# A hybrid attention step with split-precision projections: two projections at each side of the change of token groups made in pairs by halves of the contraction, and each weight load issued at its split

## The chip, the core and the metric

The program runs on one core of one Trainium2 chip, in one launch. The metric is the device time of one execution in microseconds (us). Three runs of the kernel before took 2360.5, 2361.33 and 2364.92 us; the median is 2361.33.

A core has five engines, each working through its own list of instructions in order: TensorE (PE in the profile, its weight loads PEld), VectorE (DVE), ScalarE (ACT), GpSimd (POOL) and SyncE (SP), which here only issues DMAs. An instruction that has to wait for a semaphore holds up all that stand behind it on the same engine.

## The reference

One layer over 1024 new prompt tokens and 128 sample tokens (8 streams of 16, each with 1024 cached keys and values), width 2048:

```python
h = rms_norm(x, norm_pre)
q_sb, k_sb, v_sb, gate_sb, q_r, k_r, v_r, gate_r = split(h @ w_in)   # 8 heads of 128 each
q_r, k_r = rope(q_r, pos), rope(k_r, pos) * HEAD_DIM ** -0.5
o_sb = stick_breaking(q_sb, k_sb, v_sb)      # strictly causal, over the cached keys too
o_r, state = retention(q_r, k_r, v_r, state) # chunks of 64, a decay of its own for each head
y_sb = head_rms_norm(o_sb) * silu(gate_sb)
y_r  = head_rms_norm(o_r) * silu(gate_r)
x = x + rms_norm(concat(y_sb, y_r) @ w_out, norm_post)
```

All is float32. Beside x, the new keys, values and retention states are returned.

## The kernel before, in words

**Split products.** TensorE multiplies float32 as three products of a faster format: each operand is cut in a high and a low part, and high x high, low x high and high x low are added up in the accumulator. ScalarE writes the high parts (`wh` of a weight, `mh` of the moving operand, line 138), VectorE the low parts (`wl`, `ml`, line 139). Before either can work, the raw block must have been loaded from memory: `wr` for a weight (four buffers), `mr` for an operand block (two buffers).

**Groups.** The 1152 tokens are taken in two groups. Group 0 is prompt tiles 0 to 3 and the sample tile: 640 columns, in pieces of 256 and 384. Group 1 is prompt tiles 4 to 7, 512 columns in one piece. All projections of group 0 for all eight heads come first, then all of group 1. A projection is named by what it makes and its head: q, k, v and sg (the gate) for stick-breaking, rq, rk, rv and rg for retention, so that sg7 is the last of group 0 and rq0, rk0, rv0 are the first three of group 1.

**One projection.** `project` (line 310) contracts 2048 rows in four quarters of four blocks of 128. For each quarter, called a piece here, one weight load of 256 KB is taken, split, and multiplied with that quarter of the operand: 12 products per piece and column range, 48 in all. rv and v have another form (`project_rows`: the tokens are the stationary side, the weight tiles are called `wrn`, `whn`, `wln` and the accumulators `accn`).

**The operand and its refill.** The operand of the running group stays on the chip in split form: four quarters, each with one buffer for its high and one for its low part. At the change of groups it is filled anew with group 1's normalised input, which lies in memory as `s_h`. `load_moving` (line 193) does that block by block: it issues the load of block k+1 on SP (line 199), then splits block k. A quarter can be overwritten only when the last product that reads its old content is done, and the next group's product on it waits until it is filled:

```python
            ahead = load(k + 1) if k + 1 < KT else None
            split(hi[q][:, j, at : at + n], lo[q][:, j, at : at + n], r)
```

Sixteen blocks are to be copied. sg7 takes four at its third and four at its fourth piece; rq0 takes four at its first and four at its second.

**What runs beside.** After each column of products `tick()` (line 170) lets one of the waiting jobs take a step: stick-breaking of the head before (scores `z`, `zc`, masks and scans), retention (`pa`, `pSs`), attention over the cache for the sample tokens, stores. A scheduler then settles the order of each engine's instructions, so that their place in the program is not the place in the code alone.

**Weights ahead.** `take_w` (line 278) hands out the next weight tile; it issues loads until three are in hand, the one handed out and two ahead (`W_AHEAD = 2`). The list `to_load` has them in the order of use.

**rope** (line 388) rotates rq and rk: ScalarE copies the two halves of the accumulator, swapped, into a tile `sw` (lines 392 and 393), which has one buffer, and VectorE does the arithmetic on it.

**Output.** After the heads, the output projection takes the tokens in three chunks of four panels each (`out_panel`, products in lines 1150 to 1152), with a weight load per block of 128 rows. In the third and fourth panels of a chunk the residual rows `xr` (1 MB a load, line 1197) are issued behind the newest weight load at every sixth block. The very last panel is 256 columns wide; the other 256 columns' weights have been kept on the chip before (`keep_last`, line 1176).

Of the kernel before, what the change touches and what calls it, by code (L numbers as in the profile page):

```python
# [10 lines left out]
F32R = mybir.dt.float32r  # L11
# [5 lines left out]
P = 128  # L17
# [35 lines left out]
W_AHEAD = 2  # L53
# [9 lines left out]
def tile_hybrid_step(  # L63
# [129 lines left out]
    def load_moving(mov, at, n, src):  # L193
# [10 lines left out]
        for k in range(KT):  # L204
# [14 lines left out]
            for s in (  # L219
# [5 lines left out]
    }  # L225

# [40 lines left out]
    loaded_w = []  # L267
    to_load = []
    for gi in range(2):
        for step, h in order[gi][1 - gi :]:  # L270
            if step != "ret":
                to_load += projection_loads(step, h)
# [10 lines left out]
    def load_w(first=None):  # L283
        for w in range(KT // WQ):
# [25 lines left out]
    def project(pieces, mov, loads=None, refill=()):  # L310
# [5 lines left out]
        return list(zip(acc, pieces))  # L316

# [51 lines left out]
    with ExitStack() as s1:  # L369
# [601 lines left out]
        class Head:  # L971
            def __init__(self, gi, h, last):
                self.gi, self.h, self.last = gi, h, last
                self.rest, self.ret = {}, {}
                self.sb_job = self.ret_job = None
# [13 lines left out]
            def do_rq(self):  # L989
                acc = project(self.g["pieces"], mov, run["loads"], (0, 1))  # L990
                run["loads"] = None
                if self.last:
                    drain(self.last.ret_job)
                self.ret["rq"] = rope(acc, "rq", *ropes)

            def do_rk(self):
                self.ret["rk"] = rope(project(self.g["pieces"], mov), "rk", *ropes)
# [15 lines left out]
            def do_q(self):  # L1013
# [11 lines left out]
                if self.sample:  # L1025
# [3 lines left out]
                    run["dec"] = Job(decode(self.h, qs, self.rest), D_DEC)  # L1029

            def do_k(self):
                acc = project(self.pieces, mov)
# [3 lines left out]
                ks = None  # L1036
# [4 lines left out]
                k2 = [kq.tile([P, NB_TOK], F32R, name=f"k{c}", tag=f"k{c}") for c in "hl"]  # L1041
                evac_split(acc, *k2)
                keys = [k2]
                if self.gi == 1:
# [4 lines left out]
                    keys = [old, k2]  # L1049
# [3 lines left out]
                    sb_branch(self.gi, self.tiles, self.h, self.q2, keys, kT, self.rest, ks), D_NAT[phase[0]]  # L1053
# [301 lines left out]
```

## Time and profile before

| | before |
|---|---|
| runs | 2360.5, 2361.33, 2364.92 us (median 2361.33) |
| the profiled execution: its time | 2362.25 us |
| its span, first to last instruction | 2359.5 us |
| mean granted TensorE clock | 0.997 |
| TensorE busy | 2316.6 us (98%) |
| VectorE, ScalarE, GpSimd busy | 1340.3, 895.2, 506.9 us |
| moved by DMA | 418.58 MB, mean 177 GB/s |

The views are of this one execution, and all their times count from the span's start. A row of a timeline gives start, length, engine, line, operation, out<-in, and in brackets the idle time of the engine just before with what ended it ("[3.08 <-ACT whn L138]": 3.08 us, ended by ScalarE's write of whn in line 138). A row of a windows table gives the stretch, its length and, for each engine, the busy time with its count, then the granted clock (1.00 is full), the share of the DMA engines that was busy, and GB/s. A row of groups gives busy time and the mean of one in ns.

### The profile page before, as it was taken

How to read it: one execution, taken by the hardware profiler on the slowest of the kernel's cores; microseconds unless marked ns; L12 is line 12 of the kernel's file. 1: busy time of each engine (PE TensorE's matmuls, PEld its weight loads, DVE VectorE, ACT ScalarE, POOL GpSimd, SP SyncE). 2: the span in 40 equal slices, each digit the busy share in tenths (PEclk: the TensorE clock that was granted, in tenths of full speed). 3: DMA queues.
4: the chain of work that ended last, by engine and by line, in shares of the span. 5: the costliest groups of instructions: out<-in, count | busy, mean ns of one | idle time of the engine just before them, and what ended most of it. 6: DMA issues, size and time to landing. Idle time of an engine off the chain costs nothing.

```text
span 2359.5 us, 39392 instructions
## 1 busy us (share of the span) xinstructions
PE 2316.6 (98%) x14256; PEld 2055.8 (87%) x14256; DVE 1340.3 (57%) x2689; ACT 895.2 (38%) x1926; POOL 506.9 (21%) x751
## 2 busy tenths in 40 slices
PE   7999999999999999999999999999999999999998
PEld 7999999999999999998788888888888877878887
DVE  7246564556556564557556656565665575564544
ACT  6323332333233332334343433434343444444342
POOL 3123241414223241414121211112122020010100
PEclk9999999999999999999999999999999999999999
DMA  7569686887969687797966555565565565765654
GB/s 248 151 151 232 161 187 168 190 193 174 203 147 219 170 185 178 181 209 186 231 171 151 149 159 152 140 152 156 147 160 148 146 173 187 232 213 185 202 176 132
DMA packets 697476, 418.58 MB, mean 177 GB/s; under 512 B 235072, under 2 KB 648256, under 8 KB 694848
## 3 DMA queue, kind: packets, MB, share of 16 engines
q1 hardware_dynamic: 635888, 321.12, 51.8%
q0 software_dynamic: 28304, 78.68, 13.5%
q10 hardware_dynamic: 33088, 16.26, 2.4%
q8 instruction: 111, 1.82, 0.3%
q14 instruction: 85, 0.70, 0.1%
HBM read 336.24 MB, written 79.69 MB: 176 GB/s over the span
## 4 chain that ended last, share of the span: by engine, by line
PE 84%; DMA 5%; DVE 4%; issue 4%; ACT 2%; POOL 1%; SPq 0%; ACTq 0%; DVEq 0%; POOLq 0%
PE acc L296 47%; PE accn L335 11%; PE accx L363 4%; PE a L1151 3%; PE a L1152 3%; PE a L1150 3%; PE pa L665 2%; PE z L632 2%; DMA mr<-s_y 2%; PE pd L801 1%; DMA mr<-s_ys 1%; PE zc L736 1%; DMA mr<-s_h 1%; DVE ml L139 1%; PE rs L823 1%
## 5 line engine op out<-in xcount | busy, mean ns | idle before, releaser
L139 DVE TENSOR_TENSOR wl<-wr,wh 128x512 fp32r<-128x512 f32 (+1 forms) x576 | 391.7, 683 | 514.9 <-ACT wh L138 499.9
L296 PE MATMUL acc<-mh,wl 128*128 128x256 f32 (+2 forms) x2304 | 662.9, 340 | 0.0
L296 PE MATMUL acc<-mh,wh 128*128 128x256 f32 (+2 forms) x2304 | 661.0, 339 | 0.7 <-ACT mh L138 0.7
L296 PE MATMUL acc<-ml,wh 128*128 128x256 f32 (+2 forms) x2304 | 660.4, 339 | 0.9 <-DVE ml L139 0.9
L138 ACT ACTIVATE wh<-wr 128x512 fp32r<-128x512 f32 (+1 forms) x576 | 358.8, 625 | 718.3 <-PE acc L296 397.9
L296 PEld LDWEIGHTS acc<-mh,wh 128*128 128x128 f32 x2304 | 421.4, 188 | 37.3 <-issue 6.6
L296 PEld LDWEIGHTS acc<-ml,wh 128*128 128x128 f32 x2304 | 421.3, 188 | 37.4 <-issue 6.2
L296 PEld LDWEIGHTS acc<-mh,wl 128*128 128x128 f32 x2304 | 421.1, 188 | 36.1 <-issue 7.8
L717 POOL DMA_DIRECT2D kc<-cache_sb_k x256 | 166.7, 655 | 284.4 <-DVE kcT L748 119.9
L335 PE MATMUL accn<-whn,mh 128*128 128x256 f32 x768 | 223.6, 292 | 3.1 <-ACT whn L138 3.1
L1151 PE MATMUL a<-wl,mh 128*128 128x512 f32 (+1 forms) x576 | 220.0, 382 | 2.7 <-DVE wl L139 2.5
L1150 PE MATMUL a<-wh,mh 128*128 128x512 f32 (+1 forms) x576 | 220.3, 383 | 1.8 <-ACT wh L138 1.7
L1152 PE MATMUL a<-wh,ml 128*128 128x512 f32 (+1 forms) x576 | 219.2, 381 | 0.0
L335 PE MATMUL accn<-wln,mh 128*128 128x256 f32 x768 | 217.7, 284 | 0.8 <-DVE wln L139 0.8
L335 PE MATMUL accn<-whn,ml 128*128 128x256 f32 x768 | 217.3, 283 | 0.0
L335 PEld LDWEIGHTS accn<-whn,mh 128*128 128x128 f32 x768 | 146.6, 191 | 13.8 <-issue 8.4
L575 DVE TENSOR_TENSOR_SCAN kp<-kp 128x640 f32<-128x640 f32 (+6 forms) x72 | 108.8, 1510 | 72.2 <-POOL kp L564 66.1
L335 PEld LDWEIGHTS accn<-wln,mh 128*128 128x128 f32 x768 | 147.0, 191 | 1.3 <-DVE wln L139 1.0
L335 PEld LDWEIGHTS accn<-whn,ml 128*128 128x128 f32 x768 | 146.9, 191 | 0.0
L1151 PEld LDWEIGHTS a<-wl,mh 128*128 128x128 f32 x576 | 108.3, 188 | 25.5 <-DVE wl L139 5.4
L1150 PEld LDWEIGHTS a<-wh,mh 128*128 128x128 f32 x576 | 108.3, 188 | 23.7 <-ACT wh L138 3.2
L1152 PEld LDWEIGHTS a<-wh,ml 128*128 128x128 f32 x576 | 108.3, 188 | 20.4
(206 smaller groups left out, 2984.5 us busy)
## 6 DMA issues: line engine op xcount, KB each, us to landing
wr<-w_in SPq DMA_DIRECT2D x384, 256.0 KB, 3.9
wr<-w_out SPq DMA_DIRECT2D x184, 256.0 KB, 3.5
vc<-cache_sb_v SPq DMA_DIRECT2D x64, 512.0 KB, 7.4
wrn<-w_in SPq DMA_DIRECT2D x80, 256.0 KB, 3.8
kc<-cache_sb_k SPq DMA_DIRECT2D x256, 64.0 KB, 3.9
kc<-cache_sb_k POOLq DMA_DIRECT2D x256, 64.0 KB, 4.1
wrx<-w_in SPq DMA_DIRECT2D x48, 256.0 KB, 3.1
xt<-x_prompt SPq DMA_DIRECT2D x8, 1024.0 KB, 5.3
```

The source lines that it names most:

```text
L138: nc.scalar.activation(hi, src, AF.Copy)
L139: nc.vector.tensor_tensor(lo, src, hi.bitcast(F32), ALU.subtract)
L296: last = nc.tensor.matmul(a[:, :m], lhs[:, j, :], rhs[w][:, j, o : o + m], start=(w == 0 and j == 0 and n == 0), stop=(w == KT // WQ - 1 a ...
L335: product[0] = nc.tensor.matmul(a, lhs[q][:, jj, ts], rhs[:, j, :], start=(w == 0 and j == 0 and n == 0 and t % 2 == 0), stop=(w == KT // ...
L363: product[0] = nc.tensor.matmul(banks[t], lhs[q][:, j, ts], rhs, start=(k == 0 and n == 0), stop=(k == KT - 1 and n == 2))
L575: nc.vector.tensor_tensor_scan(rev, rev, rev, 1.0, ALU.mult, ALU.bypass)
L632: mm = nc.tensor.matmul(z[:, :c], q2[a][:, i * P : (i + 1) * P], k2[b][:, :c], start=(m == 0), stop=(m == 2))
L665: nc.tensor.matmul(po[:, :P], at[:, j, :], rest["vn"][:, j, :], start=(j == 0), stop=(j == t))
L717: (nc.gpsimd if i < 2 else nc.sync).dma_start(kc[32 * i : 32 * i + 32, :].rearrange("p (k d) -> p k d", d=32), cache_k[0, 2 * c + j, s * 5 ...
L1150: nc.tensor.matmul(a[:, :width], hi[q][:, j, ts], wh, start=(k == 0), stop=False)
L1151: nc.tensor.matmul(a[:, :width], hi[q][:, j, ts], wl, start=False, stop=False)
L1152: product[0] = nc.tensor.matmul(a[:, :width], lo[q][:, j, ts], wh, start=False, stop=(k == KT - 1))
```

## The change

Three things are changed.

1. **Two pairs.** k7 and sg7 at the end of group 0, and rq0 and rk0 at the start of group 1, are each made by one new function, `project_two`: the first two pieces of the first projection, the first two of the second, the last two of the first, the last two of the second. Both keep their accumulators for that time. What followed k, rq and the start of stick-breaking is put into functions of its own (`end_k`, `end_rq`, `start_sb`), since k7 now ends ahead of sg7's last two pieces. The refill goes with it: two copies at each of the last four pieces of k7/sg7 and two at each of the first four of rq0/rk0 (`REFILL`). The list of weight loads is put in the same new order.
2. **Weight loads at their split.** `W_AHEAD` and the list of loads in hand are gone; `take_w` issues one load, and the split of that tile follows.
3. **k0 before q0** in group 1.

```diff
-W_AHEAD = 2
...
-                "rq0 rk0 rv0 rg0 ret0 q0 k0 v0 sg0 rq1 rk1 ret1 rg1 q1 k1 sg1 rq2 rk2 ret2 rg2 q2 k2 x2 sg2 "
+                "rq0 rk0 rv0 rg0 ret0 k0 q0 v0 sg0 rq1 rk1 ret1 rg1 q1 k1 sg1 rq2 rk2 ret2 rg2 q2 k2 x2 sg2 "
...
+    PAIRS = {(0, "k", 7): "sg", (1, "rq", 0): "rk"}
+    REFILL = {0: (0, 0, 0, 0, 2, 2, 2, 2), 1: (2, 2, 2, 2, 0, 0, 0, 0)}
...
+            other = PAIRS.get((gi, step, h))
+            if other:
+                skip.append((other, h))
+                a, b = projection_loads(step, h), projection_loads(other, h)
+                to_load += a[:2] + b[:2] + a[2:] + b[2:]
...
     def take_w():
-        while to_load and len(loaded_w) <= W_AHEAD:
-            loaded_w.append(to_load.pop(0)())
-        return loaded_w.pop(0)
+        return to_load.pop(0)()
...
+    def project_two(pieces, mov, loads, refill, done):
+        accs = [acc_banks(p) for p in pieces]
+        more = list(refill)
+        for half in range(2):
+            for acc, p in zip(accs, pieces):
+                for w, wh, wl in load_w(part=(2 * half, 2 * half + 1)):
+                    for _ in range(more.pop(0)):
+                        next(loads)
+                    products(mov, acc, p, w, wh, wl)
+                if half and acc is accs[0]:
+                    done(list(zip(acc, p)))
+        return list(zip(accs[1], pieces[1]))
...
             def do_rq(self):
-                acc = project(self.g["pieces"], mov, run["loads"], (0, 1))
-                run["loads"] = None
+                if (self.gi, "rq", self.h) in PAIRS:
+                    acc = project_two([self.g["pieces"]] * 2, mov, run["loads"], REFILL[1], self.end_rq)
+                    run["loads"] = None
+                    self.ret["rk"] = rope(acc, "rk", *ropes)
+                else:
+                    self.end_rq(project(self.g["pieces"], mov))
...
             def do_k(self):
-                acc = project(self.pieces, mov)
+                if (self.gi, "k", self.h) in PAIRS:
+                    self.start_loads()
+                    self.sg_acc = project_two([self.pieces] * 2, mov, run["loads"], REFILL[0], self.end_k)
+                else:
+                    self.end_k(project(self.pieces, mov))
...
             def do_sg(self):
-                if self.h == H - 1:
-                    run["after"] = [[], []]
-                    src = ((NB_TOK, from_h), (3 * P, from_y))[self.gi]
-                    run["loads"] = load_moving(run["after"], 0, *src)
-                    next(run["loads"])
-                acc = project(self.pieces, mov, run["loads"], (2, 3))
+                acc = self.sg_acc
+                if acc is None:
+                    if self.h == H - 1:
+                        self.start_loads()
+                    acc = project(self.pieces, mov, run["loads"], (2, 3))
```

How this moves the instructions is seen at three places. The rows give line, operation, out<-in and shape; the line numbers behind the change are those of the changed code, where lines 137, 399 and 412/413 are what 138, 379 and 392/393 were.

The first place is ScalarE from head 7's k to sg7's evacuation (`sg<-acc`, `gs<-acc`). The tiles mh_12985, 13066, 13148 and 13206 are the four quarters of group 1's operand before; behind the change they are mh_12838, 12987, 13130 and 13237. Before:

```order
L138 ACTIVATE mh_12985<-mr 128x512
L589 ACTIVATE sq,ssq_12494<-ro 128x128
L138 ACTIVATE mh_12985<-mr 128x512
L138 ACTIVATE wh<-wr 128x512
L867 DMA s_S_102<-S 128x128
L138 ACTIVATE mh_13066<-mr 128x512
L379 ACTIVATE sg<-acc_12845 128x256
L379 ACTIVATE sg<-acc_12846 128x256
L138 ACTIVATE mh_13066<-mr 128x512
```

Behind the change:

```order
L137 ACTIVATE kh<-acc_12642 128x256
L137 ACTIVATE kh<-acc_12643 128x256
L869 ACTIVATE ro<-pa 128x128
L137 ACTIVATE mh_12987<-mr 128x512
L609 ACTIVATE sq,ssq_12490<-ro 128x128
L137 ACTIVATE mh_12987<-mr 128x512
L887 DMA s_S_102<-S 128x128
L399 ACT_TABLE_LOAD
L399 ACTIVATE sg<-acc_12644 128x256
L399 ACTIVATE sg<-acc_12645 128x256
L137 ACTIVATE mh_13130<-mr 128x512 x2
```

Before, sg7's evacuation stands behind the first copy of the second quarter, the fifth of sixteen; now it stands behind the last copy of the second quarter, the eighth.

The second place is ScalarE at the end of rq0 and rk0, up to the weight splits of rv0 (`whn`). Before:

```order
L138 ACTIVATE mh_13206<-mr 128x512
L138 ACTIVATE wh<-wr 128x512
L138 ACTIVATE mh_13206<-mr 128x512
L558 ACTIVATE kp<-z 128x384
L559 ACTIVATE be<-z 128x384
L138 ACTIVATE mh_13206<-mr 128x512 x2
L138 ACTIVATE wh<-wr 128x512
L392 ACTIVATE sw<-acc_13141 64x512
L393 ACTIVATE sw<-acc_13141 64x512
L392 ACTIVATE sw<-acc_13351 64x512
L393 ACTIVATE sw<-acc_13351 64x512
L138 ACTIVATE whn<-wrn 128x512 x4
```

Behind the change (acc_13122 is rq0's accumulator, acc_13123 rk0's; the first `wh` here is that of rq0's third piece):

```order
L137 ACTIVATE mh_13237<-mr 128x512 x2
L137 ACTIVATE wh<-wr 128x512
L578 ACT_TABLE_LOAD
L578 ACTIVATE kp<-z 128x256
L579 ACTIVATE be<-z 128x256
L137 ACTIVATE wh<-wr 128x512 x2
L412 ACTIVATE sw<-acc_13122 64x512
L413 ACTIVATE sw<-acc_13122 64x512
L137 ACTIVATE wh<-wr 128x512
L137 ACTIVATE whn<-wrn 128x512 x3
L412 ACTIVATE sw<-acc_13123 64x512
L413 ACTIVATE sw<-acc_13123 64x512
```

The two ropes stood next to each other ahead of all of rv0's weight splits; now a split for rk0 and three for rv0 stand between them. The split of rq0's third piece stands behind the last copy.

The third place is SP in the last panel, where `wr<-w_out 128x256` are the panel's weight loads. Before:

```order
L253 DMA wr_24223<-w_out 128x256
L253 DMA wr_24238<-w_out 128x256
L253 DMA wr_24253<-w_out 128x256
L253 DMA wr_24268<-w_out 128x256
L1197 DMA xr<-x_prompt 128x2048
L253 DMA wr_24285<-w_out 128x256
```

Behind the change:

```order
L255 DMA wr_24234<-w_out 128x256
L255 DMA wr_24249<-w_out 128x256
L255 DMA wr_24264<-w_out 128x256
L1242 DMA xr<-x_prompt 128x2048
L255 DMA wr_24281<-w_out 128x256
```

The 1 MB load xr stood behind eight of the panel's weight loads and now stands behind six.

More of the change, by code (lines that the diff above doesn't have):

```diff
@@ L278, in take_w, with load_w @@
     def take_w():
-        while to_load and len(loaded_w) <= W_AHEAD:
-            loaded_w.append(to_load.pop(0)())
-        return loaded_w.pop(0)
-    def load_w(first=None):
-        for w in range(KT // WQ):
+        return to_load.pop(0)()
+    def load_w(first=None, part=range(KT // WQ)):
+        for w in part:
             wr = first[w]() if first else take_w()
@@ L996, in do_rk @@
             def do_rk(self):
-                self.ret["rk"] = rope(project(self.g["pieces"], mov), "rk", *ropes)
+                if "rk" not in self.ret:
+                    self.ret["rk"] = rope(project(self.g["pieces"], mov), "rk", *ropes)
             def do_rv(self):
@@ L1048, in do_k @@
                     split(*old, kp)
-                    keys = [old, k2]
+                    keys = [old, self.k2]
                 last = self.last
```

31 lines of the change are left out of this document (23 added, 8 removed).

## The prediction

> **What bounds the kernel now.** I read the page first, for the engine and the chain, then the windows, the timelines and the waits around the change of groups.
>
> ```profile
> span 2359.5 us, 39392 instructions
> PE 2316.6 (98%) x14256; PEld 2055.8 (87%) x14256; DVE 1340.3 (57%) x2689; ACT 895.2 (38%) x1926; POOL 506.9 (21%) x751
> PE 84%; DMA 5%; DVE 4%; issue 4%; ACT 2%; POOL 1%; SPq 0%; ACTq 0%; DVEq 0%; POOLq 0%
> ```
>
> TensorE is busy 98% of the span and is 84% of the chain that ended last. An edit that leaves its products alone can only win where TensorE stands still or runs slowly, 43 us by the page; one piece of it lies where this change works.
>
> ```profile
> 1099.50:1115.00 15.50, 15.27 (x87) 9.41 (x86) 12.66 (x31) 10.93 (x22) 6.84 (x12) 1.00 0.90 236
> 1115.00:1131.30 16.30, 14.87 (x57) 9.73 (x56) 10.46 (x18) 6.56 (x12) 7.57 (x13) 1.00 1.03 262
> 1131.30:1134.40 3.10, 0.04 (x1) 0.00 (x0) 2.85 (x6) 1.85 (x4) 0.00 (x0) 1.00 0.66 211
> ...
> 1136.00:1138.00 2.00, 2.00 (x11) 1.46 (x14) 2.00 (x5) 0.00 (x0) 0.00 (x0) 0.50 0.57 143
> 1138.00:1140.00 2.00, 2.00 (x16) 0.32 (x8) 0.36 (x2) 0.00 (x0) 0.00 (x0) 0.77 0.81 154
> ```
>
> The columns of these stretches are length, busy time of PE, PEld, DVE, ACT and POOL with counts, granted clock, DMA share, GB/s. The first two are rq0 and rk0 of group 1, with the DMA engines full (0.90 and 1.03). Then comes a hole of 3.1 us, and behind it the clock falls to 0.50. The timeline of TensorE gives the edges:
>
> ```profile
> 1099.52 0.39 PE L296 MATMUL acc<-mh,wh 128*128 128x512 f32 x1
> ...
> 1100.31 1.92 PE L736 MATMUL zc<-kcT,qp 128*32 128x512 f32 x16
> ...
> 1115.69 0.50 PE L296 MATMUL acc<-ml,wh 128*128 128x512 f32 x1 [0.49 <-DVE ml L139]
> ...
> 1125.08 0.50 PE L296 MATMUL acc<-mh,wh 128*128 128x512 f32 x1 [0.45 <-ACT mh L138]
> ...
> 1134.41 0.51 PE L335 MATMUL accn<-whn,mh 128*128 128x256 f32 x2 [3.08 <-ACT whn L138]
> 1135.68 0.58 PE L335 MATMUL accn<-wln,mh 128*128 128x256 f32 x1 [0.77 <-DVE wln L139]
> ...
> 1137.48 2.61 PE L736 MATMUL zc<-kcT,qp 128*32 128x512 f32 x16
> 1140.02 0.39 PE L335 MATMUL accn<-whn,mh 128*128 128x256 f32 x1
> ```
>
> What undisturbed work takes there is in the chain (47 products of 512 columns at a stretch) and in the groups of 1099.5 to 1131.4:
>
> ```profile
> 1304.33 10.69 PE acc L296 x47
> ...
> L736 PE MATMUL zc<-kcT,qp 128*32 128x512 f32 x16 | 1.9, 598 | 0.0
> L894 PE MATMUL pSs<-rv,rkn 32*128 32x128 f32 x16 | 1.4, 296 | 0.0
> L884 PE MATMUL pa<-st,rq 128*32 128x256 f32 x8 | 0.6, 391 | 0.0
> ```
>
> A product costs 10.69 / 47 = 0.227 us. From 1099.52 to 1134.41 (34.9 us) TensorE does 96 of them (21.8), 16 zc (1.9), 16 pSs (1.4), 8 pa (0.6) and six score products of 1920 columns in all (0.85 by the same rate): 26.6 us. **8.3 us are lost.** From 1134.41 to 1140.02 (5.6 us) stand 9 row products of 256 columns (1.0) and 16 zc (1.9): **2.7 us lost**, 0.77 of it waiting, the rest half clock. That is 11.0. Some 1.4 of it I take for changes between kinds of products, which start about 0.1 late (0.50 long instead of 0.39 above, some 14 times), and these stay. At most 9.6 us are to be had here.
>
> Two things make the loss. The first is the refill. The waits inside rq0 and rk0 end with ACT mh and DVE ml, the copies of the next group's operand:
>
> ```profile
> L138 ACT ACTIVATE mh<-mr x16: 614/632/645, 1087.0 to 1126.2; 128x512 fp32r<-128x512 f32 x16
> L139 DVE TENSOR_TENSOR ml<-mr,mh x16: 650/691/693, 1089.9 to 1126.9; 128x512 fp32r<-128x512 f32 x16
> DMA to landing us min/median/max: 2.7/3.5/4.3
> ```
>
> Sixteen copies run from 1087.0 to 1126.2, 2.6 us apart, 5.2 a pair. The pair is the unit, since mr has two buffers: copy 0.63 and 0.69, then the next load, 3.5 to land. The second is the hole before rv0:
>
> ```profile
> 1126.25 0.64 ACT L138 ACTIVATE mh<-mr 128x512 fp32r<-128x512 f32 x1 [1.22 <-DMA mr<-s_h]
> 1127.37 0.63 ACT L138 ACTIVATE wh<-wr 128x512 fp32r<-128x512 f32 x1 [0.49 <-DMA wr<-w_in]
> ...
> 1129.04 0.59 ACT L393 ACTIVATE sw<-acc 64x512 f32<-64x512 f32 x1
> 1132.51 0.59 ACT L392 ACTIVATE sw<-acc 64x512 f32<-64x512 f32 x1 [2.89 <-DVE rq L396]
> ...
> 1133.73 1.67 ACT L138 ACTIVATE whn<-wrn 128x512 fp32r<-128x512 f32 x3
> ```
>
> On ScalarE the weight splits of rv0 (whn) stand behind the second rope's sw, which waits 2.89 us for the one sw buffer that rq's rope still holds. rv0 waits for whn.
>
> **The change part by part.** *The products* stay the same in number and shape; the two pairs only reorder them. That costs nothing.
>
> *The pair k7/sg7.* It reads the first two operand quarters for the last time when half of it is done, so they can be refilled while its second half runs. In the instruction order the first four pairs of copies stand inside it, and half the operand is in when sg7 ends. Before, five copies fell into sg7's stretch (mr's own instructions in the first row, DVE and ACT, all engines in the second):
>
> ```profile
> 1082.00:1099.50 17.50, 2.80 (x5) 3.04 (x5) 1.00 0.71 182
> 1082.00:1099.50 17.50, 17.50 (x128) 17.50 (x127) 13.59 (x36) 9.97 (x26) 7.43 (x13) 1.00 0.71 182
> ```
>
> New waits inside the pair I price at zero. Its weights stand on SP ahead of the operand loads, TensorE was full in this stretch with five copies running, and DVE (13.59 of 17.50) and ACT (9.97) have room for the three more, 1.3 us a copy. If that cover fails, a pair of loads that shows costs up to its 5.2 us. What becomes late is k7's evacuation, by half of sg7, and with it head 7's stick-breaking; its score products move into rq0 and rv0, and nothing waits for them there that the order does not put behind other products.
>
> *The pair rq0/rk0.* A table load of ScalarE falls among its copies, before as in the new order; the timeline has it as
>
> ```profile
> 1109.84 1.28 ACT L147 ACT_TABLE_LOAD   x1 [0.37 <-issue]
> ```
>
> In the instruction order ScalarE makes the last four pairs of copies behind sg7's evacuation, which starts at 1099.5 as now, and the weight split of rq0's third piece behind the eighth pair. The fifth pair ends at 1099.5 + 0.7 (evacuation) + 1.3 (two copies) = 1101.5, the eighth three periods of 5.2 later, 1117.1; a table load that stands between two of the copies takes 1.28; I let half of it show, 1117.7, and the weight split adds 0.63: 1118.4. TensorE is ready for the third piece after 48 products (10.9), zc, pSs, pa and three scores (4.3) and 1.0 of changes: 1115.7. So about **2.7 us of waiting stay**, at one or two places. Then 48 products, three scores and 0.5 of changes end at 1130.3. Three whn now stand ahead of rk0's sw, and half a projection (24 products, 5.5 us) lies between the two ropes, so no hole: rv0 starts at 1130.4 against 1134.4, and without the half clock its first 2.9 + 0.3 us end at 1133.6 against 1140.0. **Gain 6.4 us.** Bounds: 9.6 if no copy is late; 3.2 if every one of the four last loads lands at 4.3 instead of 3.5 (0.8 x 4 less).
>
> The half clock followed, here, a hole of 3.08 us and a second wait of 0.77. [...]
>
> *k0 ahead of q0.* The block's job starts after the later of the two, as before: nothing, unless q0's evacuation now waits for head 7's late job; that is in the 0.5 below.
>
> *Weight loads at their split.* The instruction order of SP changes in four places only: at the start, at the change of groups, in the first heads behind it, and in the output panels. Elsewhere it is the same row for row, so two loads fewer in hand cost nothing there. At the start one x load goes ahead of two weight loads, under the products of 256 and 384 columns whose four weights are long in; uncovered, that is one landing, 3.9. In the panels the 1 MB xr loads go ahead of two weight loads each. Only in the last panel, with half-wide products, does that show now:
>
> ```profile
> wr<-w_in SPq DMA_DIRECT2D x384, 256.0 KB, 3.9
> ...
> 2315.35 0.95 SPq L1197 DMA_DIRECT2D xr<-x_prompt  x1
> ...
> 2322.48 1.43 ACT L138 ACTIVATE wh<-wr 128x256 fp32r<-128x256 f32 x4 [4.58 <-DMA wr<-w_out]
> ...
> 2322.95 0.39 PE L1150 MATMUL a<-wh,mh 128*128 128x256 f32 x1 [1.26 <-ACT wh L138]
> ```
>
> Four weight splits wait behind it and TensorE stands 1.26 us. Issued two loads earlier, it runs while the panel before is being evacuated; the wait goes, or comes two weights earlier and doubles (-1.3 to +1.3). I take -0.6, nearer to the first, because the splits stand still during that evacuation anyway. For the reordered heads of group 1 I add 0.5, one wait of the size of this row:
>
> ```profile
> 1442.57 0.49 PE L846 MATMUL pa<-S,rq 128*128 128x128 f32 x2 [0.54 <-DVE S L861]
> ```
>
> **The sum.** The profiled execution took 2362.25 us, 0.9 above the median of three, 2361.33. -6.4 - 0.6 + 0.5 = -6.5: 2355.7 beside that execution, 2354.8 beside the median, which I predict.
>
> **The rivals.**
> - *The loads run free.* The first half goes ahead of need, the loads land sooner than 3.5, and the chain of pairs is off the path: gain 9.6 and the last panel's wait, 2350.5. For it: the DMA share was 0.71 in sg7's stretch, against 1.03. Against it: the last four pairs still stand behind sg7. [...]
> - *The wait moves.* All sixteen blocks still pass two buffers, and what the hole gives back is paid in front of rq0's third piece, where no product of rk0 may run ahead any more (before, the order mixed them in). With landings of 4.3 us and another whole table load showing (1.3) the gain is 3.2 - 1.3 = 1.9: 2359.4.
> - *Slower.* SP is one queue, and weights now stand behind operand loads that wait:
>
> ```profile
> SPq L199 <- DVE ml L139: 10.0, 9, 1.8
> ```
>
> If each of the last four pairs holds up a weight load for a full turn (4.3 landing, two copies 1.3, split 1.3, 1.3 for a table load: 8.2), the eighth pair ends at 1101.5 + 3 x 8.2 = 1126 and, with the weight loads behind it landing 4.3 later, TensorE takes rq0's third piece at 1131; rv0 starts at 1143, with a half clock once more: its first products end 6 to 8 us later than now, 2368. It decides from a period of 6.2 on, where 1101.5 + 3 x 6.2 + 4.9 + 11.9 + 3.2 is 1140. Against it: nine such waits took 10.0 us in all, 1.8 at most. [...]
>
> **How the numbers follow.** The measurement tells 0.2%, 4.7 us, from no change: below 2356.6 is faster, above 2366 slower. Forecast (2352.5 to 2357.5, of which nine tenths count as faster): 0.56. Loads run free: 0.14. The wait moves: 0.21, the fringe of it faster. Slower: 0.09, of it 0.08 above 2366. Faster is 0.50 + 0.14 + 0.02 = 0.66, slower 0.08, the rest 0.26. The range 2350.5 to 2360.5 leaves out the slow case and the edges of the others.
>
> **What would show it.** Right: no idle row of about 3 us before the first accn of rv0 and the clock at 1.00 through the change of groups; mh copies beginning before sg7's last pieces and the last one near 1118; waits of one to three microseconds in all before rq0's third piece, ended by ACT wh or DVE wl; the same 98% elsewhere; no 1.26 us wait in the last panel. Wrong: waits inside k7/sg7, a wait longer than 3 us before rq0's third piece with the clock at 0.5, or new idle rows in heads 0 to 3 of group 1, where the order moved.

## The result, and the profile after

The changed kernel takes 2354.41 us (median of 12 runs, 2349.16 to 2360.09) against 2360.96 of the kernel before beside it (12 runs): a ratio of 0.9971, interval 0.9962 to 0.9981, so 6.8 us less (4.5 to 9.0). Run again later (experiment 9) it took 2352.03 against 2362.90, ratio 0.9955 (0.9944 to 0.9967). The forecast was 2354.8. The time came out as predicted. The gain does not come from where it was predicted.

The page of the changed kernel, with two of its rows of costliest groups (the last columns are idle time before them and what ended it), and the same two rows of the kernel before:

```profile
span 2354.6 us, 39387 instructions
PE 2314.7 (98%) x14256; PEld 2057.9 (87%) x14256; DVE 1341.6 (57%) x2689; ACT 895.0 (38%) x1926; POOL 512.8 (22%) x755
...
L303 PE MATMUL acc<-mh,wh 128*128 128x256 f32 (+2 forms) x2304 | 661.4, 339 | 5.6 <-ACT wh L137 5.6
...
L355 PE MATMUL accn<-whn,mh 128*128 128x256 f32 x768 | 223.4, 291 | 0.0
```

```profile
L296 PE MATMUL acc<-mh,wh 128*128 128x256 f32 (+2 forms) x2304 | 661.0, 339 | 0.7 <-ACT mh L138 0.7
...
L335 PE MATMUL accn<-whn,mh 128*128 128x256 f32 x768 | 223.6, 292 | 3.1 <-ACT whn L138 3.1
```

The hole ahead of rv0 is gone: accn, which stood idle 3.1 us for whn before, has 0.0. In its place acc<-mh,wh stands 5.6 us for ScalarE's weight split wh, where it had 0.7 for mh. The stretches of the change of groups (same columns as before):

```profile
1066.00:1082.00 16.00, 16.00 (x113) 16.00 (x112) 11.39 (x25) 5.44 (x12) 6.26 (x10) 1.00 0.73 163
1082.00:1098.10 16.10, 16.10 (x118) 16.10 (x117) 12.72 (x33) 7.40 (x21) 5.33 (x9) 1.00 0.72 193
1098.10:1116.50 18.40, 15.05 (x82) 8.89 (x80) 12.02 (x28) 10.49 (x22) 7.84 (x14) 1.00 0.83 207
1116.50:1133.00 16.50, 14.09 (x53) 10.70 (x53) 10.06 (x19) 8.00 (x14) 8.10 (x13) 0.90 0.99 244
1133.00:1140.00 7.00, 6.83 (x45) 4.83 (x46) 5.88 (x11) 3.54 (x8) 1.28 (x2) 1.00 0.71 189
```

The first two are the pair k7/sg7, with TensorE full. In the next two, rq0/rk0, it lacks 3.35 and 2.41 us and the clock is at 0.90 in the second; in the last, rv0, 0.17. Its timeline has the waits:

```profile
1105.31 0.50 PE L303 MATMUL acc<-mh,wh 128*128 128x512 f32 x1 [1.28 <-ACT wh L137]
...
1116.47 0.50 PE L303 MATMUL acc<-mh,wh 128*128 128x512 f32 x1 [2.07 <-ACT wh L137]
...
1122.13 0.50 PE L303 MATMUL acc<-mh,wh 128*128 128x512 f32 x1 [2.23 <-ACT wh L137]
...
1139.13 0.39 PE L355 MATMUL accn<-whn,mh 128*128 128x256 f32 x1
```

They stand ahead of the second piece of rq0, the second of rk0 and the third of rq0, 5.6 us in all. The last row answers to 1140.02 before: rv0's tenth row product. It comes 0.9 earlier, but this execution was 1.0 ahead already at 1008 us, before the change of groups begins. **At the change of groups this execution gained nothing.**

ScalarE and SP, in the same stretch, show what the splits wait for:

```profile
1100.34 1.16 ACT L137 ACTIVATE mh<-mr 128x512 fp32r<-128x512 f32 x2
...
1104.63 0.63 ACT L137 ACTIVATE wh<-wr 128x512 fp32r<-128x512 f32 x1 [1.66 <-DMA wr<-w_in]
...
1111.87 0.63 ACT L137 ACTIVATE mh<-mr 128x512 fp32r<-128x512 f32 x1 [2.85 <-DMA mr<-s_h]
...
1113.87 1.28 ACT L146 ACT_TABLE_LOAD   x1 [1.37 <-DVE kcT L768]
...
1115.28 0.61 ACT L137 ACTIVATE mh<-mr 128x512 fp32r<-128x512 f32 x1
1115.80 0.61 ACT L137 ACTIVATE wh<-wr 128x512 fp32r<-128x512 f32 x1
...
1119.92 0.63 ACT L137 ACTIVATE mh<-mr 128x512 fp32r<-128x512 f32 x1 [1.95 <-DMA mr<-s_h]
1121.45 0.63 ACT L137 ACTIVATE wh<-wr 128x512 fp32r<-128x512 f32 x1 [0.91 <-DMA wr<-w_in]
```

```profile
1095.25 2.31 SPq L198 DMA_DIRECT2D mr<-s_h  x2
1097.61 0.42 SPq L737 DMA_DIRECT2D kc<-cache_sb_k  x1
1098.09 0.48 SPq L236 DMA_DIRECT2D wr<-w_in  x1
...
1116.65 0.33 SPq L198 DMA_DIRECT2D mr<-s_h  x1
1117.02 0.43 SPq L236 DMA_DIRECT2D wr<-w_in  x1
```

The first wait is for a weight load that SP could only issue at 1098.09, behind a pair of operand loads, and that then took 6.5 us to land (3.9 is the median of these loads). The second is a split that stands behind a copy, which stands behind a table load. The third is a weight load behind the very last operand load. In the last panel the other thing to see is when xr goes, and what ScalarE's splits there wait for (2300 to 2335 us):

```profile
2308.32 0.43 SPq L1242 DMA_DIRECT2D xr<-x_prompt  x1
```

```profile
2316.71 0.42 ACT L137 ACTIVATE wh<-wr 128x256 fp32r<-128x256 f32 x1 [0.72 <-DMA wr<-w_out]
```

xr went at 2315.35 before and goes 7.0 us earlier now; no split waits more than 0.9 for its weight there (4.58 before), and TensorE not at all.

To see where the time went in every kernel, take the start of the same TensorE product in each and subtract its start in the profile before. The marks are zn at 1007.94 us in the kernel before, pd at 1038.09, zn at 1141.54 (inside rv0), the last accx at 1830.02, the panels' products a at 2312.90 and 2332.01, and the end at 2359.51. Each column is what a stretch adds (minus is faster):

| profile | to 1008 | to 1038 | change of groups, to 1142 | heads, to 1830 | panels, to 2313 | last panel, to 2332 | end | span |
|---|---|---|---|---|---|---|---|---|
| the change | -1.0 | 0.0 | +0.1 | -0.2 | -0.9 | -2.2 | -0.8 | -5.0 |
| 9, the change again | -0.8 | -1.6 | -0.9 | -0.2 | -2.7 | -2.2 | -0.8 | -9.1 |
| 3, two loads in hand in the panels | -2.6 | -1.6 | +0.6 | +0.3 | +0.6 | -0.8 | -0.1 | -3.6 |
| 10, q0 first | -1.1 | -1.6 | +2.0 | +0.2 | +0.2 | -2.2 | -0.2 | -2.7 |
| 1, two loads in hand throughout | -0.9 | -1.6 | +5.3 | -0.2 | -0.7 | -1.1 | -0.7 | 0.0 |
| 2, loads at their split alone | -0.9 | -1.6 | +2.0 | +0.2 | -2.8 | -2.2 | -0.5 | -5.7 |
| 5, the same in the panels alone | +0.2 | -0.4 | +2.1 | 0.0 | -2.2 | -2.2 | -0.1 | -2.5 |
| 6, own tile for rk0's rope | -1.3 | -0.1 | +1.8 | 0.0 | +1.7 | -0.7 | +0.2 | +1.6 |
| 4, copies spread | -0.2 | -1.5 | -0.8 | -0.2 | -1.4 | -2.2 | -0.3 | -6.6 |
| 7, spread, one load in hand | -1.1 | -1.6 | -1.5 | -0.2 | -1.3 | -2.2 | -0.1 | -7.9 |
| 8, refill a piece earlier | -2.7 | -1.6 | -2.0 | 0.0 | -1.3 | -2.2 | -0.3 | -10.0 |
| 11, early, four copies late | -1.2 | -1.6 | +0.5 | +0.2 | +0.9 | -2.2 | -0.3 | -3.7 |
| 12, one operand load | -0.4 | -0.4 | -7.2 | -0.6 | -3.4 | -2.2 | -0.8 | -14.9 |

Up to 1008 us the ten kernels with loads at their split there (the change, 9, 3, 10, 2, 4, 7, 8, 11 and 12) give TensorE the same order of instructions, and yet they lie between -0.2 and -2.7: 2.5 us are chance in one execution. At the change of groups the order of the changed kernel was seen four times (the change, 9, 3 and 10: +0.1, -0.9, +0.6, +2.0, mean 0.4), that of the kernel before twice (0 and 5: +2.1, mean 1.1).

### The profile page after: what moved, and what is told of

Same layout as the page of the kernel before. It is cut to its first block, busy times and chain, and to the rows that moved or that the text cites. A ratio compares the mean times of both kernels' runs of the same rounds, so it can differ in the third digit from the quotient of the medians.

```text
span 2354.6 us, 39387 instructions
## 1 busy us (share of the span) xinstructions
PE 2314.7 (98%) x14256; PEld 2057.9 (87%) x14256; DVE 1341.6 (57%) x2689; ACT 895.0 (38%) x1926; POOL 512.8 (22%) x755
## 4 chain that ended last, share of the span: by engine, by line
PE 87%; DMA 5%; DVE 3%; issue 2%; ACT 2%; SPq 0%; POOL 0%; DVEq 0%; ACTq 0%; POOLq 0%
PE acc L303 49%; PE accn L355 11%; PE accx L383 5%; PE a L1196 3%; PE a L1197 3%; PE a L1195 3%; DMA mr<-s_y 3%; PE pa L685 3%; PE z L652 2%; PE pd L821 1%; PE zc L756 1%; DVE ml L138 1%; DMA wr<-w_in 1%; DMA mr<-s_ys 1%; PE rs L843 1%
```

## The experiments

All times are medians; the ratio is to the kernel before on the same chip.

**1. The pairs without the loads at their split.**

```diff
     def take_w():
-        return to_load.pop(0)()
+        while to_load and len(loaded_w) <= W_AHEAD:
+            loaded_w.append(to_load.pop(0)())
+        return loaded_w.pop(0)
```

(with `W_AHEAD = 2` and the list of loads in hand back)

> The change with its two weight loads in hand put back: pairs, refill and k0 before q0 stay, only the loads at their split are undone. Theory P (the pairs pay, as predicted: 6.4 us at the change of groups): about 6 us faster than the kernel before, and no wait of about 1.3 us in the last panel removed. Theory L (the profile of the change: its pairs gained about nothing from 1037 to 1172 us, the gain lies in loads issued at their split, in the output panels above all): within 2 us of the kernel before, the 1.26 us wait of the last panel back.

2362.74 against 2361.61, ratio 1.000 (0.9991 to 1.0008). The pairs alone gain nothing; the change of groups is even 5.3 us worse in the profile. TensorE's waits there:

```profile
1120.62 0.50 PE L307 MATMUL acc<-mh,wh 128*128 128x512 f32 x1 [3.47 <-ACT wh L138]
...
1134.75 0.50 PE L359 MATMUL accn<-whn,mh 128*128 128x256 f32 x2 [2.22 <-ACT whn L138]
...
1137.77 0.58 PE L359 MATMUL accn<-wln,mh 128*128 128x256 f32 x1 [2.52 <-DVE wln L139]
```

With two loads in hand, the second rope stands ahead of all whn on ScalarE again, and the hole ahead of rv0 is back (2.22 and 2.52) beside the new wait in rq0. So the pairs alone do not remove the hole. The wait in the last panel did not come back in full, as the second theory had it: TensorE stood 0.19 there, and the stretch gained 1.1 of the 2.2.

**2. The loads at their split without the pairs.**

```diff
-W_AHEAD = 2
+W_AHEAD = 0
```

(in the kernel before)

> The kernel before with weight loads issued at their split and nothing else changed. Theory P: within 1 us of the kernel before. Theory L: 4 to 6 us faster, with the last panel free of its wait and with the hole of 3.1 us ahead of rv0 and its half clock still there.

2357.49 against 2361.61, ratio 0.9981 (0.9972 to 0.9989): 4.5 us, two thirds of the 6.8 of the change, with none of the pairs. That is within the range of the second theory. Its profile gains in the panels (-2.8 and -2.2), not at the change of groups (+2.0). One part of the expectation failed: the hole of 3.1 us ahead of rv0 is not there. TensorE and ScalarE:

```profile
1116.89 0.80 PE L296 MATMUL acc<-mh,wh 128*128 128x512 f32 x1 [3.49 <-ACT wh L138]
```

```profile
1131.90 1.65 ACT L138 ACTIVATE whn<-wrn 128x512 fp32r<-128x512 f32 x3
1137.07 0.59 ACT L392 ACTIVATE sw<-acc 64x512 f32<-64x512 f32 x1 [3.52 <-PE acc L296]
```

Three whn stand ahead of rk0's rope, as in the change, and no product of rv0 waits for whn. So it is the loads at their split that put whn ahead and remove the hole, with or without the pairs. In its place this kernel has other waits in rq0 and rk0, the longest of 3.49 us, and a mean granted clock of 0.92 from 1100 to 1142 us, where the kernel before has 0.96.

**3. The change with two loads in hand in the panels.** As in 1, but only once the output panels' loads begin.

> The change, but with two weight loads in hand again once the output panels begin; up to there it is the change itself. Theory P: about 6 us faster than the kernel before, 0.6 less than the change. Theory L: 1 to 2.5 us faster, with the last panel's wait of 1.3 back and some 2 us lost again between 2090 and 2140 us. Up to 1930 us it is a second look at the change: three waits for a weight split of 1.3, 2.1 and 2.2 us in rq0 and rk0 and a half clock behind them, if these belong to the order and not to one execution.

2356.66 against 2361.61, ratio 0.9978 (0.9968 to 0.9989). In time this is 5.2 us faster (2.6 to 7.6), nearer the 6 of the first theory than the 2.5 at most of the second. The profile speaks for the second: the panels' gain is gone (+0.6, and -0.8 in place of -2.2), the change of groups gains nothing (+0.6), and rq0/rk0 had waits of 2.07, 0.21 and 2.45 us. The two are not reconciled.

**5. The kernel before with the loads at their split in the panels alone.**

```diff
-        while to_load and len(loaded_w) <= W_AHEAD:
+        while to_load and len(loaded_w) <= (0 if len(to_load) <= 12 * KT + 2 else W_AHEAD):
```

> The kernel before, with weight loads issued at their split in the output panels alone; the heads and the change of groups keep two loads in hand, no pairs. If the gain of the change lies in the panels (from 2098 us on the change runs ahead of the kernel before by 1.9 us up to 2133 and by 2.2 more up to 2332): 3 to 5 us faster than the kernel before, both pieces there again, and up to 1930 us nothing but chance. If it lies in the loads of the heads, or in the pairs: within 1.5 us of the kernel before.

2358.62 against 2361.61, ratio 0.9989 (0.9981 to 0.9998): 2.6 us (0.5 to 4.5), a little under the 3 to 5 expected. Both pieces are there: -2.2 in the panels up to 2313 and -2.2 in the last. The change of groups is that of the kernel before, and took 2.1 us more in this execution than in the first: its 3.1 us hole was 3.22 here, and the waits in rq0 and rk0 were longer.

**9. The change again.** No edit.

> The changed kernel once more, unaltered, for a second profile of its change of groups. If the three waits of 1.3, 2.1 and 2.2 us and the half clock belong to its order of instructions: waits of the same sizes within 1 us at rq0's second, rk0's second and rq0's third piece, ended by ScalarE's weight split, and at least one window of half clock. If they were chance of one execution: under 3 us of waits in all and no half clock. Last panel without a wait in either case; 5 to 8 us faster than the kernel before.

2352.03 against 2362.90, ratio 0.9955 (0.9944 to 0.9967), 10.6 us, more than the 5 to 8 expected.

```profile
1114.65 0.50 PE L303 MATMUL acc<-mh,wh 128*128 128x512 f32 x1 [2.95 <-ACT wh L137]
...
1119.89 0.50 PE L303 MATMUL acc<-mh,wh 128*128 128x512 f32 x1 [0.42 <-ACT wh L137]
...
1130.78 0.50 PE L303 MATMUL acc<-mh,wl 128*128 128x512 f32 x1 [1.57 <-DVE wl L138]
```

The sum is 4.9 (5.6 in the first profile, 4.7 in run 3, 6.7 in run 10, which has the same order there), with half clock again: the mean granted clock from 1100 to 1142 us is 0.96, as in the first profile. Its division changes with the execution, further than expected. The first wait was absent: its weight load landed in 4.8 us here, where it took 6.5 in the first profile. And the third of these rows stands at another place, rk0's last piece, with another cause, on VectorE:

```profile
1128.24 0.71 DVE L768 STREAM_TRANSPOSE kcT<-kc 128x512 f32<-128x512 f32 x1 [3.41 <-issue]
...
1130.04 0.68 DVE L138 TENSOR_TENSOR wl<-wr,wh 128x512 fp32r<-128x512 f32 x1
```

The weight split stands behind the transpose of a block of cached keys, whose load GpSimd had issued at 1123.81 and which landed 4.3 us later. Runs 3 and 10 have 2.45 and 2.44 us at this place, the first profile 0.20. So the order of the change has a fourth wait, which is for neither the operand nor a weight load, though it too is gone in run 12.

**4. The copies of rq0/rk0 spread.** One at each of the first four pieces, four at the fifth.

```diff
-    REFILL = {0: (0, 0, 0, 0, 2, 2, 2, 2), 1: (2, 2, 2, 2, 0, 0, 0, 0)}
+    REFILL = {0: (0, 0, 0, 0, 2, 2, 2, 2), 1: (1, 1, 1, 1, 4, 0, 0, 0)}
```

> The change with rq0/rk0's eight copies put one at each of the first four pieces and four at the fifth, in place of two at each of the first four, so that rq0's third piece, which reads the third quarter of the operand only, no longer stands behind the copies of the fourth. If the wait at that place (2.2 us in the change) comes from the split and the weight load standing behind the last copies, it falls below 0.7 or moves to the fourth piece as at most 1.5, no half clock follows, and the time is 2 to 4 us below the change. If the copies themselves are the bound (16 blocks through two buffers), the same 2 us stand ahead of the fourth piece and the time is that of the change.

2356.03, ratio 0.9974 (0.9965 to 0.9984). The wait ahead of rq0's third piece fell to 0.22; ahead of its fourth stood 3.99, longer than either theory had it, and again with half clock (0.96 on the mean from 1100 to 1142 us, as in the change):

```profile
1122.84 0.80 PE L303 MATMUL acc<-mh,wh 128*128 128x512 f32 x1 [3.99 <-ACT wh L137]
```

```profile
1116.83 0.34 SPq L198 DMA_DIRECT2D mr<-s_h  x1
1117.23 1.03 SPq L236 DMA_DIRECT2D wr<-w_in  x2
```

The fourth piece's weight load was issued right behind the last operand load. So one more trial:

**7. Spread, with one weight load in hand inside rq0/rk0.**

```diff
+                    in_hand[0] = 1
                     acc = project_two([self.g["pieces"]] * 2, mov, run["loads"], REFILL[1], self.end_rq)
+                    in_hand[0] = 0
```

(take_w then issues loads while `len(loaded_w) <= in_hand[0]`)

> The change with rq0/rk0's copies one at each of the first four pieces and four at the fifth, and, within rq0/rk0 only, one weight load in hand, so that no weight load stands on SP behind the last operand loads. In the spread copies without it a wait of 3.99 us stood ahead of rq0's fourth piece, for a weight load issued behind two operand loads. If that queueing is the cause: this wait falls below 1.5 us, no half clock, 2 to 3 us faster than the change. If the copies are the bound: a wait of 2 to 4 us stands there still, ended by ACT mh or DVE ml, and the time is that of the change.

2354.27 (5 runs), ratio 0.9968 (0.9956 to 0.9981). The weight is no longer late, and the wait stays:

```profile
1123.21 0.79 PE L307 MATMUL acc<-mh,wh 128*128 128x512 f32 x1 [3.88 <-ACT mh L137]
```

It stands inside rq0's fourth piece, ahead of its last block, and is ended by the copy itself now. The last operand load was issued at 1117.87 and landed 4.6 us later. With the weight's queueing away, the pace of the operand loads is what is left at this place.

**8. The refill begun a piece earlier.** `REFILL = {0: (0, 0, 0, 2, 2, 2, 2, 2), 1: (1, 1, 1, 1, 2, 0, 0, 0)}`, one load in hand as in 7.

> As the run before, but the refill begins one piece earlier (ten copies inside k7/sg7, one at each of rq0/rk0's first four pieces and two at the fifth). If the pace of the copies (two buffers, about 5 us a pair) is what is left, they end about 4 us earlier against TensorE and the change of groups loses 4 to 6 us less than in the change: 2348 to 2351. If the copies go no faster inside k7/sg7, because their loads stand behind the cached keys on SP, waits of 1 to 3 us stand at sg7's last piece instead and the time is that of the change.

2355.52, ratio 0.9974 (0.9964 to 0.9984). The 2348 to 2351 expected did not come. The profile was the shortest with all operand loads (2349.5, -2.0 at the change of groups), the median was not. Waits of 1.18 (ahead of rq0's first piece, for its weight), 1.14 (rk0's second) and 1.94 us (rk0's third) stay. The last has yet another cause on ScalarE:

```profile
1120.72 0.59 ACT L416 ACTIVATE sw<-acc 64x512 f32<-64x512 f32 x1 [3.26 <-PE acc L307]
...
1121.94 1.15 ACT L137 ACTIVATE wh<-wr 128x512 fp32r<-128x512 f32 x2
```

rk0's third weight split stands behind rq0's rope, which waits for rq0 to end.

**11. The same with the last four copies at the fifth piece.** `1: (1, 1, 0, 0, 4, 0, 0, 0)`.

> The early refill with one weight load in hand, with its last six copies put one at each of rq0/rk0's first two pieces and four at the fifth. In the instruction order of ScalarE the weight split of rk0's third piece then stands ahead of rq0's rope; in the run before it stood behind it, and TensorE waited 1.94 us and went to half clock. If that place was the cause: no wait of over 1.5 us in rk0, no half clock, and the change of groups 3 us shorter than there. If the four copies at the fifth piece are late instead: a wait of 2 to 4 us ahead of rq0's fourth piece, and nothing gained.

2356.01, ratio 0.9969 (0.9957 to 0.9982). Nearest the second outcome: 1.88 us ahead of the last block of rq0's fourth piece for ACT mh, and 1.06, 1.06 and 1.63 elsewhere. Nothing gained.

**12. Fifteen of the sixteen operand loads left out.**

```diff
-            ahead = load(k + 1) if k + 1 < KT else None
+            ahead = r if n == NB_TOK else load(k + 1) if k + 1 < KT else None
```

> The change with fifteen of the sixteen operand loads of the change of groups left out: all sixteen copies are still made, from the one block that is loaded, so group 1 computes with a wrong operand. What it tells: whether the waits in rq0 and rk0 come from the loads (their landing, their two buffers, and the weight loads that stand behind them on SP) or from the copies and the jobs on ScalarE and VectorE. If the loads: under 1.5 us of waits in all in rq0 and rk0, no half clock, and the stretch from 1038 to 1142 us 4 to 7 us shorter than in the change. If the engines: 3 us of waits or more stay, ended by ScalarE or VectorE.

2347.80, ratio 0.9944 (0.9932 to 0.9956). The same windows of the changed kernel and of this one:

```profile
1100.00:1133.00 33.00, 27.24 (x125) 18.73 (x113) 21.58 (x45) 16.99 (x35) 14.20 (x24) 0.95 0.91 225
```

```profile
1100.00:1133.00 33.00, 32.52 (x188) 24.38 (x181) 24.85 (x52) 17.80 (x37) 15.20 (x26) 1.00 0.80 191
```

All sixteen copies are still made, from the one block that is loaded, and TensorE lacks 0.5 us in place of 5.8; the change of groups is 7.3 us shorter than in the first profile of the change, the clock stays at 1.00. The waits come from the loads, not from the copies or the jobs. (Without the loads the order on ScalarE shifts somewhat too, and the DMA engines are less full, 0.80 in place of 0.91. The run does not part the landing of a load from the queueing behind it, nor either from the other loads' share of the DMA engines. Runs 4 and 7 part queueing from landing at one place.)

**6. A tile of its own for rk0's rope,** in the kernel before.

```diff
-                sw = ep.tile([P, 512], F32, name="sw", tag="sw", bufs=1)
+                sw = own or ep.tile([P, 512], F32, name="sw", tag="sw", bufs=1)
...
+                own = wp.tile([P, 512], F32, name="swk", tag="mr", bufs=2) if (self.gi, self.h) == (1, 0) else None
```

> The kernel before, with a tile of its own for the rope of rk0 in group 1 (one of the two mr buffers, free by then), so that its copy on ScalarE no longer waits 2.89 us for rq0's rope. If the hole ahead of rv0 came from that one buffer, as the prediction has it: rv0's first weight splits come about 3 us earlier, no wait over 1 us and no half clock there, 4 to 5 us faster. If the hole was the refill's lateness in another form, another wait stands at the same place and less than 2 us are gained.

2361.28, ratio 0.9997 (0.9988 to 1.0006): nothing. The second outcome. rk0's rope no longer waits for VectorE, but for rk0's own last product, and the whn behind it wait with it:

```profile
1131.12 0.59 ACT L392 ACTIVATE swk<-acc 64x512 f32<-64x512 f32 x1 [1.79 <-PE acc L296]
...
1132.34 2.19 ACT L138 ACTIVATE whn<-wrn 128x512 fp32r<-128x512 f32 x4
```

TensorE stood 1.94 and 1.50 us, in place of 3.08 and 0.77, and the mean granted clock from 1100 to 1142 us was 0.92, in place of 0.96. The hole was the place of whn behind the rope on an engine that works in order; the single buffer only ended the wait last.

**10. q0 before k0 again,** in the change.

> The change with q0 before k0 in group 1, as it was. If the 0.65 us that the changed kernels gain between the end of rv0's heads and 1830 us come from k0 before q0: the wait of 0.53 us at about 1442 (for VectorE's S) is back and the step from 1232 to 1830 us is within 0.1 of the kernel before. If they come from the pair: the step stays at -0.65. In time no more than 1 us to the change.

2355.67, ratio 0.9971 (0.9960 to 0.9982). The wait at 1442 is back, on the microsecond:

```profile
1442.13 0.49 PE L866 MATMUL pa<-S,rq 128*128 128x128 f32 x2 [0.53 <-DVE S L881]
```

From 1232 to 1830 us this kernel gains 0.01, the change 0.65; but from 1142 to 1232 the change gives 0.45 back and this one 0.15. k0 first is worth some 0.3 us net in these two executions, and 0.2 in the means of the table's column of the heads (nine with k0 first, five without). In time this kernel lay 3.6 us above the change beside it (run 9), where at most 1 was expected; five and six runs do not settle whether that is more than chance.

## Why the prediction was right in its time and wrong in its reasons

That the time came out within 0.4 us was luck: the largest term failed, and terms that stood at nothing or had the wrong sign made up for it.

**The sum, term by term** (predicted; then what the profiles show, as the mean of the executions that have the order in question):

- *Change of groups: -6.4; measured -0.6* (0.4 in four executions against 1.1 in two, with 2 to 3 us between single ones). This is the step that failed. Even with that chance, 6.4 is far outside. Of the rivals, "the wait moves" (a gain of 1.9, a chance of 0.21) comes nearest in size; in form it was the third, as told below.
- *Last panel: -0.6; measured -1.5.* The ten profiles with loads at their split there have -2.2 each, and no wait; the four with two loads in hand have 0, -1.1, -0.8 and -0.7, mean -0.7. The mechanism was right (xr ahead of two weight loads), the size too small: I counted the 1.26 us of idle time in one row, and not the slower spacing behind it.
- *The other panels: 0; measured about -1.7* (-1.3 over the nine profiles with loads at their split, run 12 left aside, +0.4 over the four others; single executions lie up to 2 us off). "Only in the last panel does that show now" was too narrow. Short waits for weight splits stand there. All four executions with two loads in hand have them (0.48, 0.23 and 0.30 us between 2101 and 2123 before). Of those with loads at their split, 9, 2 and 5 have none, the first profile of the change one of 0.20, but 4 and 7 have 0.5 and 1.0, and 8, 10 and 11 still 1.9 to 2.6 us. So the waits become rarer and do not go for good; why is not shown.
- *Reordered heads: +0.5; measured -0.2.* The wait whose size I borrowed for a new one, at 1442, is the one that went.

That makes -4.0, against 6.8 (4.5 to 9.0) in time. By the same means (ten executions with loads at their split there, four without), the stretches to 1008 and to 1038 us add -0.7 and -0.8, which I had at nothing. The first is within what chance does there. The second is the wait ahead of pd near 1038 us (0.9 to 1.4): it stands in all three executions of the old order of the heads with two loads in hand and no pairs (before, 5, 6), in the first of the change, and in run 12 (0.96), but in none of the other nine. Nothing in the order of instructions near it tells me why.

The times ask for more than these rows show. Run 3, without the panels' gain, was still 5.2 us faster. The change, measured again, gained 10.6 us (7.8 to 13.2) against 4.5 (2.6 to 6.6) of run 2, which has the loads at their split and neither pairs nor k0 first. In the first measurement of the change the difference to run 2 was 2.3 us and inside the intervals. So the pairs together with loads at their split may be worth some 2 to 6 us that single profiles put into no one place. That is open.

**What held.** The pair k7/sg7 has no wait: TensorE is busy 16.00 of 16.00 us from 1066 and 16.10 of 16.10 from 1082. Eight blocks were in when sg7 ended, and the fifth pair ended at 1100.34 + 1.16 = 1101.5, as worked out. The hole ahead of rv0 went because whn stand ahead of rk0's rope, as worked out; runs 1 and 6 show the same from the other side. But I put that down to the pair, and it is the work of the loads at their split: run 2 has it without the pair, and run 1, with the pair alone, does not.

**Where it broke.** "The eighth three periods of 5.2 later." The copies of the last pairs end at 1101.5, 1108.5, 1115.9 and 1120.55: periods of 7.0, 7.4 and 4.7, mean 6.35. In 9, 3 and 10 the mean is 5.8, 5.9 and 6.1. I took the period from a row that averaged over quiet stretches, and the copies' own chain only. Three things can be seen in the longer turns of the first profile. The two loads of the sixth pair landed in 4.3 and 4.5 us, in place of 3.5. In the seventh a copy whose load had landed at 1114.17 began at 1115.28, behind the table load, which showed whole, with 1.37 of waiting ahead of it, where I let half of it show. And copies now stand on ScalarE behind weight splits, which wait for weight loads, which wait on SP behind operand loads, which wait for copies; the copy at 1106.61 stands behind a split that waited 1.66 for its load. No run tells the shares of the three apart. And I looked for the waiting at rq0's third piece alone, while the first two waits, 3.35 us, fell ahead of it, where weight splits were late and not the operand. So 5.6 us of waits stood in place of 2.7, and the granted clock was 0.50 from 1122.53 to 1125.94 us.

The third rival had the right form. It named this queue, and a period of 6.2 from which the gain is gone: 1101.5 + 3 x 6.2 + 4.9 + 11.9 + 3.2. With 6.35 the same sum gives 1140.6; measured was 1139.13 in an execution that was 1.0 ahead, 1140.1. I gave it 0.09 because nine such waits had taken only 10.0 us before the change, at most 1.8 each. But that row described the old order, in which weight loads were issued two ahead of need. The new order of the copies lengthens the period even then: run 1 has two weight loads in hand, and its last three periods are 4.9, 6.3 and 7.2, mean 6.1. So the loads at their split, which I had priced at nothing there, are not the whole of it.

**The bound.** At most 9.6 us was to be had, by the forecast. Run 12 shows 7.2 without the loads. None of the four other placements of the copies (4, 7, 8, 11) came out clearly faster than the change in time: 2354.27 to 2356.01 against 2354.41 and 2352.03.

## What to carry to other kernels

A wait that stands on an in-order queue has a place, not an owner: taking away what ended it last (run 6) or moving the work it delayed (runs 4, 7, 8, 11) hands it to the next instruction in the queue, unless what feeds the queue is taken away (run 12). Price a chain through several queues by its whole turn in the new order, not by the old order's median, and ask which slack of the old order the same change takes away. And a forecast can hit the time with its main term wrong: only parts run alone (1, 2, 5) told that the main edit gains nothing by itself, and that 4.5 us of the 6.8 to 10.6 came with an edit I had priced at a tenth of the whole.

## What the runs showed of the hardware

The granted clock fell to 0.50 behind some waits of TensorE and not behind others. Stretches that follow one another (columns as above, granted clock third from the end), first in run 8, then in run 5, then in run 6:

```profile
1119.63:1123.04 3.41, 1.47 (x7) 0.85 (x5) 1.40 (x3) 2.28 (x4) 2.72 (x4) 1.00 0.78 241
1123.05:1126.46 3.41, 3.02 (x8) 2.08 (x7) 3.17 (x6) 1.16 (x3) 0.68 (x2) 0.50 1.06 275
```

```profile
1120.25:1123.66 3.41, 1.60 (x8) 1.11 (x6) 1.63 (x4) 0.45 (x2) 0.77 (x1) 1.00 1.00 228
1123.67:1127.08 3.41, 2.96 (x13) 2.46 (x14) 2.10 (x3) 1.68 (x4) 1.97 (x5) 1.00 0.77 148
```

```profile
1966.44:1969.85 3.41, 2.41 (x11) 1.67 (x9) 1.41 (x3) 1.46 (x3) 0.00 (x0) 1.00 0.44 150
1969.86:1973.27 3.41, 1.76 (x12) 1.62 (x13) 3.37 (x6) 0.94 (x2) 0.00 (x0) 1.00 0.37 120
1973.27:1976.68 3.41, 3.41 (x21) 2.94 (x20) 3.17 (x9) 0.97 (x3) 0.00 (x0) 1.00 0.52 166
```

In run 8 TensorE was idle for 1.94 us of the first stretch, and the clock was 0.50 in the second. In run 5 it was idle for 1.81 us of the first, and the clock was 1.00 in the second. In run 6 a single wait of 2.67 us, longer than the idle time in either, lies across the first two rows (1.00 and 1.65 us idle), and the clock was 1.00 in all three. The idle times rest on modelled ends of the products. So 1.94 us of idle time stood ahead of a half clock in one execution, and a wait of 2.67 us ahead of none in another; what decides it, these rows do not show. By my estimate from the row at 0.50, one such stretch moves an execution by 1.7 us, half of its 3.41.
